# Layer 0 of a hybrid decoder trunk: one block transpose, bonus weights and memory norm in the projection stage, retention scores in banks of two pools

## The chip, the cores and the metric

The kernel runs on one NeuronCore of a Trainium2 chip. The metric is the device time of one execution in microseconds (us), lower is better. Three timed runs of the kernel before gave 912.21, 913.45 and 913.68 us; the median is 913.45 us.

## The reference, cut to what matters

A trunk of two layers over 256 tokens of width 1024. Each layer adds a mixer, a cross-attention into 256 memory tokens and a squared-ReLU MLP; the memory is normalized once, for both layers.

```python
mem_n = rms_norm(mem, mem_norm_w)
h = x
for layer in range(2):
    hn = rms_norm(h, norm_mix_w[layer])
    if layer % 2 == 0:
        proj = hn @ hyb_w_in[i]                       # 1792 columns for A, 2048 for B
        y_a = rwkv7_time_mix(proj[..., :A_COLS], ...)
        y_b = retention(proj[..., A_COLS:], ret_ln_w[i])
        mix = concatenate([y_a, y_b]) @ hyb_w_out[i]
    else:
        mix = diff_attention(hn, ...)
    h = h + mix
    h = h + memory_cross_attention(rms_norm(h, ...), mem_n, ...)
    h = h + squared_relu_mlp(rms_norm(h, ...), ...)
return rms_norm(h, final_norm_w)

def rwkv7_time_mix(pa, ...):                          # 8 heads of 64
    pa = pa + (token_shift(pa) - pa) * mu             # r, k, v, wd, ad, gd are columns of pa
    decay = exp(-exp(-softplus(-(w0 + tanh(wd) @ w2)) - 0.5))
    a = sigmoid(a0 + ad @ a2)
    kk = (k * k_k) / max(norm(k * k_k), 1e-12)        # per head
    k = k * (1 + (a - 1) * k_a)
    y = wkv7_scan(r, decay, k, v, -kk, kk * a)
    y = group_norm(y) + sum(r * k * r_k) * v          # the bonus
    return y * (sigmoid(gd) @ g2)

def retention(pb, ln_w):                              # 8 heads of 64, chunks of 128
    q, k, v, g = split(pb, 4)
    q, k = rotary(q), rotary(k) / 8
    scores = (q @ k.T) * decay_mask                   # inside a chunk; a state crosses chunks
    return rms_norm(scores @ v + cross) * silu(g)
```

## The kernel before, in words

All matrices with weights are multiplied in three passes: a weight piece of 512 KB (`raw`) is loaded by SyncE's queue, ScalarE makes its rounded half `hi` and VectorE the rest `lo` (line 129, `split`), and TensorE multiplies both by the activations' halves (line 121, `mm`). There are four `raw`, three `hi` and three `lo` buffers, so TensorE lets pieces in by finishing older ones.

A tile framework puts every engine's instructions into one fixed order, by priorities and the order of the code; each engine then runs its row of instructions in that order and waits by semaphores. PSUM has eight banks: four in the pool `acc`, two in `mm`, two in `tr`.

Layer 0's mixer, in the order of the code:

- **Start**: `x` is loaded, normalized and transposed to `xT`; the transposes need the identity in `prm` (line 94).
- **Projection stage** (`proj_cols`, seven pairs of blocks): r, k, v, the low-rank inputs; evacuated by `shift_mix`.
- **Vector work of A**: the decays `Ep`, `En`, the vectors `AR`, `bt`, `kt`, the product `rk = r*k` on GpSimd (line 480), its weights `rkb` on GpSimd (line 499), and the bonus `bv` (lines 502 to 505), whose matmul needs both.
- **Projections of B** (`proj_rows` into `acc` banks): k and q with rotary evacuations `rope_evac`, then v, then the gate g.
- **Scores of A** (`scores`): matmuls of `bt` with `AR` in four groups through the `tr` banks, masked by VectorE into `SCb`.
- **Inverse** (`inverse`): the 32x32 diagonal blocks of `SCb` are transposed into `Lc` (line 573, one operation for each quarter of 32 partitions, since the column of the block alternates), scaled by `D2c` (line 576), and inverted by 31 steps of a product and an addition (lines 583, 585), scaled and transposed to `X` (line 588). The recurrence (`solve`) needs `X`.
- **Scores of B** (lines 597 to 617): for four pairs of heads, matmuls of `kTr` and `qTr` into two banks (`ps`, `ps1`), both from `tr`; VectorE masks and ScalarE copies them out to `PT0`, `PT1`.
- **Memory norm** (`load_mem`, called after `inverse`): its weight row is loaded on ScalarE's queue, both memory tiles on SyncE's, squared by ScalarE, scaled by VectorE, transposed by TensorE into `memh`, `meml`.
- **Recurrence of A**: four steps `g`, each a chain over TensorE, VectorE and ScalarE; matmuls of the first cross-attention's keys and values (`kv_chunk`, fed by `memh`, `meml`) are put between.

Of the kernel before, what the change touches and what calls it, by code (L numbers as in the profile page):

```python
# [8 lines left out]
F32 = mybir.dt.float32  # L9
F32R = mybir.dt.float32r  # L10
AF = mybir.ActivationFunctionType
ALU = mybir.AluOpType
# [4 lines left out]
D = 1024  # L17
# [12 lines left out]
R_W0, R_A0, R_KK, R_KA, R_LW, R_LB, R_RK, R_MU, R_RET, R_DIF = (  # L30
    0, 4, 8, 12, 16, 20, 24, 28, 42, 46)
# [6 lines left out]
def kernel(ctx: ExitStack, tc: tile.TileContext, ins: dict, out: bass.AP):  # L38
    nc = tc.nc
    I = ins  # L40
# [5 lines left out]
    const = ctx.enter_context(tc.tile_pool(name="const", bufs=1))  # L46
# [10 lines left out]
    def open_pool(name, side=None):  # L57
        st = ExitStack()
        return st, st.enter_context(tc.tile_pool(name=name, bufs=1, side=side, reuse_waits="tile"))
# [15 lines left out]
    def mm_t():  # L75
        return ps_mm.tile([128, 512], F32, tag="mm", name=nm("mm"))

    def tr_t():
        return ps_tr.tile([128, 512], F32, tag="tr", name=nm("tr"))


    h = glob.tile([128, 2, D], F32, tag="h", name="h")
# [10 lines left out]
    prm = const.tile([128, C_ALL], F32, name="prm")  # L93
# [3 lines left out]
    blk1 = prm[:, C_BO:C_BO + 128]  # L97
# [147 lines left out]
    def scratch():  # L245
        return npool.tile([128, D], F32, tag="xn", name=nm("xn"))
# [45 lines left out]
    def load_row(tl, src, eng):  # L292
        eng.dma_start(out=tl, in_=src.unsqueeze(0).broadcast_to([128, D]))
        return [tl[:, 0:512], tl[:, 512:1024]]
# [33 lines left out]
    def load_mem(pool):  # L328
        mh = pool.tile([128, 8, 256], F32R, tag="memh", name="memh")
        ml = pool.tile([128, 8, 256], F32R, tag="meml", name="meml")  # L330
        row = load_row(kv1pool.tile([128, 2, D], F32, tag="V1", name="memrow")[:, 0, :], I["mem_norm_w"], nc.scalar)

        def src(t):
            mt = scratch()
            nc.sync.dma_start(out=mt, in_=I["mem"][0, t * 128:(t + 1) * 128, :])
            return mt
        norm_T(src, row, mh, ml, (tr_t, tr_t))
        return mh, ml

    def kv_chunk(layer, i, KT, V, between=None):  # L340

        if i < 4:
            def ev(ps):
                if layer == 0:
                    nc.vector.tensor_copy(out=KT[:, 2 * i:2 * i + 2, :], in_=ps)
                else:
                    split(KT[0][:, 2 * i:2 * i + 2, :], KT[1][:, 2 * i:2 * i + 2, :], ps)
            proj_cols(I["w_k"][layer], 2 * i, memT, ev, between=between)
        else:
            c = i - 4  # L350
            proj_rows(I["xattn_w_kv"][layer], D + c * 512, memT,
                      lambda ps, t: nc.scalar.activation(V[:, t, c * 512:(c + 1) * 512], ps, AF.Copy), mm_t)
# [6 lines left out]
    omu = const.tile([128, 14], F32, name="omu")  # L359
    behind(nc.vector.tensor_scalar(omu, prm[:, R_MU:R_MU + 14], -1.0, 1.0, op0=ALU.mult, op1=ALU.add), d1[1], "the activations first")  # L360
    oka = const.tile([128, 4], F32, name="oka")
    const.tile([128, 24], F32, name="pad")
    behind(nc.vector.tensor_scalar(oka, prm[:, R_KA:R_KA + 4], -1.0, 1.0, op0=ALU.mult, op1=ALU.add), d1[1], "the activations first")

    st_pr, prep = open_pool("prep", "right")
    w2a2 = prep.tile([128, 512], F32, tag="w2a2", name="w2a2")

# [3 lines left out]
    r_ = t4(prep, "r")  # L371
# [23 lines left out]
    for b0 in (12, 4, 6, 0, 2, 8, 10):  # L395
        if b0 == 6:
            nc.sync.dma_start(out=w2a2[0:64, :], in_=I["rwkv_w2"][0])
            nc.sync.dma_start(out=w2a2[64:128, :], in_=I["rwkv_a2"][0])
            nc.sync.dma_start(out=prm[:, C_BO:C_ALL], in_=I["c_pack"][:, C_BO:C_ALL])
        if b0 == 8:  # L400
            nc.sync.dma_start(out=g2, in_=I["rwkv_g2"][0])
            nc.sync.dma_start(out=rkt.rearrange("p a t c -> p (a t c)"), in_=I["c_rk"])
        def ev(ps, b0=b0):
            for j in range(2):
                shift_mix(ps[:, j, :], b0 + j)
        proj_cols(I["w_hyb"], b0, xT, ev)

    sg = t4(prep, "sg")  # L410
# [59 lines left out]
    nc.vector.tensor_tensor(kk, kk, a_, op=ALU.mult)  # L470
    nc.vector.tensor_tensor(bt, g16(kk), En, op=ALU.mult)
    for b in range(4):
        nc.vector.tensor_scalar(a_[:, b, :], a_[:, b, :], prm[:, R_KA + b:R_KA + b + 1], oka[:, b:b + 1],
                                op0=ALU.mult, op1=ALU.add)
    nc.vector.tensor_tensor(k_, k_, a_, op=ALU.mult)
    kt_ = pA.tile([128, 16, 64], F32, tag="kt", name="kt")
    nc.vector.tensor_tensor(kt_, g16(k_), En, op=ALU.mult)
    nc.vector.tensor_tensor(AR[:, :, 1, :], g16(r_), Ep[:, :, 1:65], op=ALU.mult)
    rk = r_
    nc.gpsimd.tensor_tensor(rk, r_, k_, op=ALU.mult)  # L480


    def tok_major(src, tag):
# [10 lines left out]
    kT = tok_major(kt_.rearrange("p (b g) t -> p b (g t)", b=4), "kT")  # L494


    rkb = prep.tile([128, 4, 128], F32, tag="sg", name="rkb")
    for b in range(4):
        nc.gpsimd.tensor_scalar(rkb[:, b, :], blk1, prm[:, R_RK + b:R_RK + b + 1], None, op0=ALU.mult)
    bv = v_  # L500
    for b0 in (0, 2):
        ps = tr_t().rearrange("p (b t) -> p b t", b=2)
# [4 lines left out]

    st_rp, rp = open_pool("rp")
    st_pr.close()
    st_mem, mempool = open_pool("mem", "right")  # L510
    st_kv1, kv1pool = open_pool("kv1", "right")
    st_pB, pB = open_pool("pB", "right")
    qkR = [rp.tile([128, 2, 512], F32, tag=f"qk{i}", name=f"qkR{i}") for i in range(2)]
# [10 lines left out]
    def rope_evac(i):  # L524
        def ev(ps, t):
            p4 = ps.rearrange("p (h x d) -> p h x d", h=8, x=2)
            cs, sn = rope_tabs(i, t)
            dst = qkR[i][:, t, :].rearrange("p (h x d) -> p h x d", h=8, x=2)
            tm = scratch()[:, :512].rearrange("p (h x d) -> p h x d", h=8, x=2)
            for x in range(2):  # L530
                nc.vector.tensor_tensor(dst[:, :, x, :], p4[:, :, x, :], cs, op=ALU.mult)
                nc.vector.tensor_tensor(tm[:, :, x, :], p4[:, :, 1 - x, :], sn, op=ALU.mult)
            nc.vector.tensor_tensor(dst[:, :, 0, :], dst[:, :, 0, :], tm[:, :, 0, :], op=ALU.subtract)
            nc.vector.tensor_tensor(dst[:, :, 1, :], dst[:, :, 1, :], tm[:, :, 1, :], op=ALU.add)
        return ev

    wh_in = I["hyb_w_in"][0]
# [28 lines left out]
    def inverse():  # L566

        Lc = pB.tile([128, 32, 32], F32, tag="Lc", name="Lc")
        SCb16 = SCb.rearrange("p a h t -> p (a h) t")
        for q in range(4):  # L570
            pr = slice(q * 32, q * 32 + 32)
            c0 = (q % 2) * 32
            nc.vector.transpose(Lc[pr].rearrange("p t s -> p (t s)"),  # L573
                                SCb16[pr, :, c0:c0 + 32].rearrange("p h t -> p t h").unsqueeze(2)
                                .broadcast_to([32, 32, 2, 16]))
        nc.vector.tensor_tensor(Lc, Lc, D2c.unsqueeze(1).broadcast_to([128, 32, 32]), op=ALU.mult)
        Xc = pB.tile([128, 32, 16], F32, tag="Xc", name="Xc")
        behind(nc.sync.dma_start(out=Xc.rearrange("p s m -> p (s m)"), in_=I["c_xi"]), last_load[0], "weights first")
        for k in range(31, 0, -1):
            m0 = k // 2  # L580
            n = 16 - m0
            pd = pB.tile([128, 32, 16], F32, tag="pd", name=nm("pd"), bufs=1)
            nc.vector.tensor_tensor(pd[:, 0:k, 0:n], Lc[:, k, 0:k].unsqueeze(2).broadcast_to([128, k, n]),
                                    Xc[:, k:k + 1, m0:16].broadcast_to([128, k, n]), op=ALU.mult)
            nc.vector.tensor_tensor(Xc[:, 0:k, m0:16], Xc[:, 0:k, m0:16], pd[:, 0:k, 0:n], op=ALU.add)
        nc.vector.tensor_tensor(Xc, Xc, D2p.unsqueeze(1).broadcast_to([128, 32, 16]), op=ALU.mult)
        X = pB.tile([128, 16, 32], F32, tag="pd", name="X")
        nc.vector.transpose(X.rearrange("p h (m par) -> p m par h", par=2), Xc.rearrange("p s m -> p m s"))
        Xt[0] = X
# [11 lines left out]
    for hq in range(2):  # L601
        p0 = rp.tile([128, 4, 256], F32, tag=f"qk{hq}", name=nm("PT0"))
        p1 = PT1[hq]
        PT0.append(p0)
        for h2 in range(2):
            pr = slice(h2 * 64, h2 * 64 + 64)
            ps = tr_t().rearrange("p (h c) -> p h c", h=2)
            ps1 = tr_t()[:, :256].rearrange("p (h c) -> p h c", h=2)
            for i in range(2):
                hp = 2 * hq + i  # L610
                mm(ps[:, i, :], lhsT=kTr[pr, hp, 0:128], rhs=qTr[pr, hp, :], start=True, stop=True)
                mm(ps1[:, i, :], lhsT=kTr[pr, hp, 128:256], rhs=qTr[pr, hp, 128:256], start=True, stop=True)
            d0 = p0.rearrange("p (i h) c -> p h i c", i=2)[:, h2]
            d1 = p1.rearrange("p (i h) c -> p h i c", i=2)[:, h2]
            nc.vector.tensor_tensor(d0[:, :, 0:128], ps[:, :, 0:128], cmb, op=ALU.mult)
            nc.scalar.activation(d0[:, :, 128:256], ps[:, :, 128:256], AF.Copy)
            nc.vector.tensor_tensor(d1, ps1, cmb, op=ALU.mult)
# [3 lines left out]
        nc.vector.tensor_tensor(gR[:, t, :], ps, gR[:, t, :], op=ALU.mult)  # L621

    inverse()
    memT = load_mem(mempool)
    proj_rows(wh_in, A_COLS + 1536, xT, g_evac, acc_t)
    pos = []
    for t in range(2):
# [671 lines left out]
```

## Time and profile before

| | us |
|---|---|
| median of three runs | 913.45 |
| the profiled execution | 913.95 |
| its span on the core | 912.1 |
| TensorE busy in the span | 885.7 |
| VectorE busy | 601.0 |
| ScalarE busy | 450.7 |
| mean granted TensorE clock | 0.983 of 2.4 GHz |

Times in the views are microseconds from the span's start. "PE" is TensorE's matmuls, "PEld" its weight loads, DVE is VectorE, ACT ScalarE, POOL GpSimd, SP the queue that issues loads. A releaser is the instruction whose end let a waiting one start. A PE that is marked busy can still run slowly: the column PEclk gives the granted share of 2.4 GHz, and 0.50 is 1.2 GHz.

### The profile page before, as it was taken

To read this page: it belongs to the slowest core of one execution; us is meant where nothing else is said; L and a number is where in the kernel's file an instruction comes from. 1 tells how busy PE (TensorE), PEld (TensorE's weight loads), DVE (VectorE), ACT (ScalarE), POOL (GpSimd) and SP (SyncE) were. 2 spreads that over 40 slices of the span, in tenths; PEclk is the share of its full clock that TensorE was granted. 3 is DMA by queue.
4 is the path that set the end of the run, shared out by engine and by line. 5 is a ranking of instruction groups with operands and counts; after the bars stand their busy time and mean duration, and the time that the engine had idled before them with its cause. 6 is when DMAs were issued, how large, how long until landed. Compare 5 with 4: busy or idle time off the path is not lost.

```text
span 912.1 us, 14133 instructions
## 1 busy us (share of the span) xinstructions
PE 885.7 (97%) x5546; PEld 757.8 (83%) x5546; DVE 601.0 (66%) x954; ACT 450.7 (49%) x721; POOL 34.9 (4%) x44
## 2 busy tenths in 40 slices
PE   7998989999999999999999999999999999999996
PEld 5986869877889988888888889878899788888885
DVE  4568868745558557666666674887776666666665
ACT  4754425213556445544444454665465454444443
POOL 1003001000000000000000000001000000000001
PEclk8999969999999999999999999999999999999999
DMA  8544523222465565655655555444453465656551
GB/s 295 183 139 150 162 72 121 87 94 76 134 217 202 155 194 194 197 188 191 193 191 186 189 181 187 138 131 147 139 208 105 127 207 185 189 192 195 187 187 67
DMA packets 47078, 149.98 MB, mean 164 GB/s; under 512 B 4731, under 2 KB 4900, under 8 KB 46884
## 3 DMA queue, kind: packets, MB, share of 16 engines
q1 hardware_dynamic: 45456, 142.73, 48.4%
q10 hardware_dynamic: 1108, 3.72, 1.2%
q0 software_dynamic: 448, 2.63, 0.9%
q8 instruction: 43, 0.70, 0.3%
q14 instruction: 23, 0.19, 0.1%
HBM read 148.01 MB, written 2.63 MB: 165 GB/s over the span
## 4 chain that ended last, share of the span: by engine, by line
PE 89%; DVE 5%; issue 2%; ACT 2%; POOL 1%; DMA 1%; SPq 0%; POOLq 0%; ACTq 0%; DVEq 0%
PE mm L121 37%; PE acc L121 34%; PE tr L121 15%; DVE lo L129 1%; ACT hi L129 1%; DVE Lc L573 1%; DMA prm<-in_c_pack_dram 1%; PE tr L254 1%; PE tr L1104 1%; PE tr L951 1%; DVE z L1085 0%; PE acc L254 0%; DVE xn L268 0%; POOL xn L1182 0%; POOL rs L226 0%
## 5 line engine op out<-in xcount | busy, mean ns | idle before, releaser
L129 DVE TENSOR_TENSOR lo<-raw,hi 128x1024 fp32r<-128x1024 f32 x262 | 320.1, 1224 | 220.9 <-ACT hi L129 219.1
L129 ACT ACTIVATE hi<-raw 128x1024 fp32r<-128x1024 f32 x262 | 277.5, 1060 | 345.6 <-PE mm L121 130.3
L121 PE MATMUL mm<-xhl,hi 128*128 128x256 f32 (+1 forms) x784 | 188.0, 319 | 1.0 <-ACT xhl L129 0.7
L121 PEld LDWEIGHTS mm<-xhl,hi 128*128 128x128 f32 x784 | 129.6, 189 | 11.9 <-ACT xhl L129 1.7
L121 PE MATMUL mm<-xhl,lo 128*128 128x256 f32 x512 | 138.1, 282 | 0.0
L121 PE MATMUL acc<-hi,hl 128*128 128x512 f32 x256 | 100.2, 391 | 0.0
L121 PE MATMUL acc<-hi,hh 128*128 128x512 f32 x256 | 100.1, 391 | 0.0
L121 PE MATMUL acc<-lo,hh 128*128 128x512 f32 x256 | 99.6, 389 | 0.0
L121 PEld LDWEIGHTS mm<-xhl,lo 128*128 128x128 f32 x512 | 96.6, 189 | 2.5
L121 PE MATMUL tr<-xhl,hi 128*128 128x512 f32 x256 | 92.8, 395 | 0.0
L121 PE MATMUL acc<-hi,xhl 128*128 128x512 f32 x256 | 81.9, 396 | 0.0
L121 PE MATMUL tr<-xhl,lo 128*128 128x256 f32 x256 | 66.7, 281 | 0.0
L121 PEld LDWEIGHTS acc<-hi,hl 128*128 128x128 f32 x256 | 48.1, 188 | 11.3 <-DVE hl L129 0.9
L121 PEld LDWEIGHTS acc<-lo,hh 128*128 128x128 f32 x256 | 48.1, 188 | 10.4
L121 PEld LDWEIGHTS acc<-hi,xhl 128*128 128x128 f32 x256 | 47.7, 188 | 9.7
L121 PEld LDWEIGHTS acc<-hi,hh 128*128 128x128 f32 x256 | 48.1, 188 | 8.8
L121 PEld LDWEIGHTS tr<-xhl,hi 128*128 128x128 f32 x256 | 48.2, 188 | 8.5
L121 PEld LDWEIGHTS tr<-xhl,lo 128*128 128x128 f32 x256 | 48.2, 188 | 2.9
L121 PE MATMUL acc<-lo,xhl 128*128 128x512 f32 x128 | 50.4, 394 | 0.0
L121 PE MATMUL mm<-memh,hi 128*128 128x256 f32 x128 | 36.5, 286 | 1.3 <-ACT xhl L132 1.3
L121 PE MATMUL mm<-meml,hi 128*128 128x256 f32 x128 | 37.1, 290 | 0.0
L121 PE MATMUL mm<-memh,lo 128*128 128x256 f32 x128 | 36.6, 286 | 0.0
(299 smaller groups left out, 1393.3 us busy)
## 6 DMA issues: line engine op xcount, KB each, us to landing
raw<-in_w_dram SPq DMA_DIRECT2D x64, 512.0 KB, 3.5
raw<-in_mlp_w_dram SPq DMA_DIRECT2D x64, 512.0 KB, 3.5
raw<-in_hyb_w_in_dram SPq DMA_DIRECT2D x16, 512.0 KB, 3.8
raw<-in_w_k_dram SPq DMA_DIRECT2D x16, 512.0 KB, 3.5
raw<-in_xattn_w_kv_dram SPq DMA_DIRECT2D x16, 512.0 KB, 3.4
raw<-in_w_q_dram SPq DMA_DIRECT2D x16, 512.0 KB, 4.4
raw<-in_xattn_w_o_dram SPq DMA_DIRECT2D x16, 512.0 KB, 3.4
raw<-in_w_dqk_dram SPq DMA_DIRECT2D x16, 512.0 KB, 3.4
```

The costliest lines, as they stand in the source:

```text
L121: ins = nc.tensor.matmul(o, lhsT=lhsT, rhs=rhs, start=start, stop=stop)
L129: return nc.scalar.activation(hi, src, AF.Copy), nc.vector.tensor_tensor(lo, src, r32(hi), op=ALU.subtract)
L254: nc.tensor.transpose(ps[:, k4, :], x[:, kt * 128:(kt + 1) * 128], ident)
L573: nc.vector.transpose(Lc[pr].rearrange("p t s -> p (t s)"), SCb16[pr, :, c0:c0 + 32].rearrange("p h t -> p t h").unsqueeze(2) .broadcast_t ...
L951: nc.tensor.transpose(pt[:, j, m, :], P[:, j, m * 128:(m + 1) * 128], ident)
L1104: nc.tensor.transpose(pt[:, k * 128:(k + 1) * 128], z3[:, 0, k * 128:(k + 1) * 128], ident)
```

## The change

Six edits, all in layer 0, with the same result for the kernel's output:

1. `load_mem` is called inside the projection stage, behind the fourth pair of blocks, and the memory's weight row goes to a buffer of the pool `prep` that is free from the start. The pool `mem` is opened earlier.
2. `rkb` is made by GpSimd inside the projection stage; `rk = r*k` moves from GpSimd to VectorE.
3. The scaling of `a` by k_a (four operations) moves from VectorE to ScalarE; so do the four copies that evacuate the keys of the first cross-attention (`KT`).
4. The rotary evacuation has one multiplication of 512 columns in place of two of 256 and one addition in place of two; the sign is folded into the sine products.
5. In `inverse` ScalarE and VectorE first gather the diagonal blocks into `Ld` with two masks of ones and zeros (`quad`), and one transpose of 128 partitions replaces four of 32.
6. In the scores of B `ps` comes from the pool `mm`, `ps1` from `tr` as before.

```diff
@@ load_mem
-        row = load_row(kv1pool.tile([128, 2, D], F32, tag="V1", name="memrow")[:, 0, :], I["mem_norm_w"], nc.scalar)
+        row = load_row(prep.tile([128, D], F32, tag="kk", name="memrow"), I["mem_norm_w"], nc.scalar)
@@ kv_chunk
-                    nc.vector.tensor_copy(out=KT[:, 2 * i:2 * i + 2, :], in_=ps)
+                    nc.scalar.activation(KT[:, 2 * i:2 * i + 2, :], ps, AF.Copy)
...
+    quad = const.tile([128, 2], F32, name="quad")
+    for q in range(4):
+        for j in range(2):
+            nc.gpsimd.memset(quad[q * 32:q * 32 + 32, j:j + 1], float(q % 2 == j))
...
+    st_mem, mempool = open_pool("mem", "right")
     st_pr, prep = open_pool("prep", "right")
@@ the loop over b0 of the projection stage
         proj_cols(I["w_hyb"], b0, xT, ev)
-
+        if b0 == 0:
+            memT = load_mem(mempool)
+        if b0 == 2:
+
+            rkb = prep.tile([128, 4, 128], F32, tag="rkb", name="rkb")
+            for b in range(4):
+                nc.gpsimd.tensor_scalar(rkb[:, b, :], blk1, prm[:, R_RK + b:R_RK + b + 1], None, op0=ALU.mult)
...
-        nc.vector.tensor_scalar(a_[:, b, :], a_[:, b, :], prm[:, R_KA + b:R_KA + b + 1], oka[:, b:b + 1],
-                                op0=ALU.mult, op1=ALU.add)
+        nc.scalar.activation(a_[:, b, :], a_[:, b, :], AF.Identity, scale=prm[:, R_KA + b:R_KA + b + 1],
+                             bias=oka[:, b:b + 1])
...
-    nc.gpsimd.tensor_tensor(rk, r_, k_, op=ALU.mult)
+    nc.vector.tensor_tensor(rk, r_, k_, op=ALU.mult)
...
-    rkb = prep.tile([128, 4, 128], F32, tag="sg", name="rkb")
-    for b in range(4):
-        nc.gpsimd.tensor_scalar(rkb[:, b, :], blk1, prm[:, R_RK + b:R_RK + b + 1], None, op0=ALU.mult)
@@ rope_evac
+            nc.vector.tensor_tensor(dst, p4, cs.unsqueeze(2).broadcast_to([128, 8, 2, 32]), op=ALU.mult)
             for x in range(2):
-                nc.vector.tensor_tensor(dst[:, :, x, :], p4[:, :, x, :], cs, op=ALU.mult)
-                nc.vector.tensor_tensor(tm[:, :, x, :], p4[:, :, 1 - x, :], sn, op=ALU.mult)
-            nc.vector.tensor_tensor(dst[:, :, 0, :], dst[:, :, 0, :], tm[:, :, 0, :], op=ALU.subtract)
-            nc.vector.tensor_tensor(dst[:, :, 1, :], dst[:, :, 1, :], tm[:, :, 1, :], op=ALU.add)
+                nc.vector.scalar_tensor_tensor(tm[:, :, x, :], p4[:, :, 1 - x, :], 2.0 * x - 1.0, sn,
+                                               op0=ALU.mult, op1=ALU.mult)
+            nc.vector.tensor_tensor(dst, dst, tm, op=ALU.add)
@@ inverse
-        for q in range(4):
-            pr = slice(q * 32, q * 32 + 32)
-            c0 = (q % 2) * 32
-            nc.vector.transpose(Lc[pr].rearrange("p t s -> p (t s)"),
-                                SCb16[pr, :, c0:c0 + 32].rearrange("p h t -> p t h").unsqueeze(2)
-                                .broadcast_to([32, 32, 2, 16]))
+
+        Ld = pB.tile([128, 16, 32], F32, tag="pd", name="Ld", bufs=1)
+        nc.scalar.activation(Ld, SCb16[:, :, 0:32], AF.Identity, scale=quad[:, 0:1])
+        nc.vector.scalar_tensor_tensor(Ld, SCb16[:, :, 32:64], quad[:, 1:2], Ld, op0=ALU.mult, op1=ALU.add)
+        nc.vector.transpose(Lc.rearrange("p t s -> p (t s)"),
+                            Ld.rearrange("p h t -> p t h").unsqueeze(2).broadcast_to([128, 32, 2, 16]))
@@ scores of B
-            ps = tr_t().rearrange("p (h c) -> p h c", h=2)
+            ps = mm_t().rearrange("p (h c) -> p h c", h=2)
             ps1 = tr_t()[:, :256].rearrange("p (h c) -> p h c", h=2)
...
     inverse()
-    memT = load_mem(mempool)
     proj_rows(wh_in, A_COLS + 1536, xT, g_evac, acc_t)
```

The edits also move instructions of each engine. First place: VectorE from the third mask of A's scores to the first masks of B's scores (`PT`). `xn`, `memrow` belong to the memory norm, `lo` to the weight pieces, `pd` and `Xc` to the 31 steps. Before:

```order
L562 TENSOR_TENSOR SCb<-tr_1029,prm 128x512
L268 SCALAR_TENSOR_TENSOR xn_1263<-xn_1261,rs_1270,memrow 128x512
L573 STREAM_TRANSPOSE Lc<-SCb 32x1024
L129 TENSOR_TENSOR lo_1319<-raw_1317,hi_1318 128x1024
L573 STREAM_TRANSPOSE Lc<-SCb 32x1024 x2
L129 TENSOR_TENSOR lo_1337<-raw_1335,hi_1336 128x1024
L573 STREAM_TRANSPOSE Lc<-SCb 32x1024
L129 TENSOR_TENSOR lo_1355<-raw_1353,hi_1354 128x1024
L615 TENSOR_TENSOR PT_142_1115<-tr_1116,prm 128x2x128
L617 TENSOR_TENSOR PT_795<-tr_1117,prm 128x2x128
L576 TENSOR_TENSOR Lc<-Lc,D2c 128x1024
```

and after (in two pieces; between them stand the rest of the first four pairs of `pd` and `Xc`, rows of the same kind):

```order
L570 TENSOR_TENSOR SCb<-tr_1088,prm 128x512
L581 SCALAR_TENSOR_TENSOR Ld<-SCb,quad,Ld 128x512
L582 STREAM_TRANSPOSE Lc<-Ld 128x1024
L129 TENSOR_TENSOR lo_1320<-raw_1318,hi_1319 128x1024
L584 TENSOR_TENSOR Lc<-Lc,D2c 128x1024
L129 TENSOR_TENSOR lo_1338<-raw_1336,hi_1337 128x1024
L591 TENSOR_TENSOR pd_1220<-Lc,Xc 128x31
L593 TENSOR_TENSOR Xc<-Xc,pd_1220 128x31
```

```order
L593 TENSOR_TENSOR Xc<-Xc,pd_1229 128x28x2
L129 TENSOR_TENSOR lo_1356<-raw_1354,hi_1355 128x1024
L623 TENSOR_TENSOR PT_156_1174<-mm_1175,prm 128x2x128
L625 TENSOR_TENSOR PT_862<-tr_1176,prm 128x2x128
L623 TENSOR_TENSOR PT_156_1174<-mm_1184,prm 128x2x128
L625 TENSOR_TENSOR PT_862<-tr_1185,prm 128x2x128
```

Four transposes became one, the scaling of `Lc` and four pairs of steps moved ahead of the first masks, and two pairs of heads are masked in a row.

Second place: TensorE around the first two pairs of heads of B's scores (`acc` are the matmuls of the gate's projection). Before, the second pair comes eleven `acc` matmuls behind the first:

```order
L121 MATMUL acc_1040<-hi_1096,xl_124 128x512
L121 MATMUL tr_1116<-qkT_793,qkT_794 128x256
L121 MATMUL tr_1117<-qkT_793,qkT_794 128x128
L121 MATMUL tr_1116<-qkT_793,qkT_794 128x256
L121 MATMUL tr_1117<-qkT_793,qkT_794 128x128
L121 MATMUL acc_1315<-hi_1318,xh_123 128x512
```

and after, two pairs follow each other, then three `acc` matmuls, then the other two pairs:

```order
L121 MATMUL acc_1099<-hi_1155,xl_124 128x512
L121 MATMUL mm_1175<-qkT_860,qkT_861 128x256
L121 MATMUL tr_1176<-qkT_860,qkT_861 128x128
L121 MATMUL mm_1175<-qkT_860,qkT_861 128x256
L121 MATMUL tr_1176<-qkT_860,qkT_861 128x128
L121 MATMUL mm_1184<-qkT_860,qkT_861 128x256
L121 MATMUL tr_1185<-qkT_860,qkT_861 128x128
L121 MATMUL mm_1184<-qkT_860,qkT_861 128x256
L121 MATMUL tr_1185<-qkT_860,qkT_861 128x128
L121 MATMUL acc_1316<-hi_1319,xh_123 128x512
L121 MATMUL acc_1316<-lo_1320,xh_123 128x512
L121 MATMUL acc_1316<-hi_1319,xl_124 128x512
```

What moved: the four pairs are packed into two bunches, and a third pair meets a bank that the first one still holds.

Third place: SP's queue of loads in the projection stage (`xn` are the memory tiles). After:

```order
L144 DMA raw_336<-in_w_hyb_dram 128x1024
L335 DMA xn_469<-in_mem_dram 128x1024
L144 DMA raw_366<-in_w_hyb_dram 128x1024
L144 DMA raw_401<-in_w_hyb_dram 128x1024
L144 DMA raw_431<-in_w_hyb_dram 128x1024
L335 DMA xn_496<-in_mem_dram 128x1024
L144 DMA raw_524<-in_w_hyb_dram 128x1024
```

Before, the two memory loads stood among the gate's weights, some twenty loads later; the load of `memrow`, which was behind `kT`'s copies on ScalarE's queue, is now the first instruction of that queue.

## Rows read from the trace of the kernel before

**Rows 1.** The page, busy us of each engine (share) and count.
```profile
PE 885.7 (97%) x5546; PEld 757.8 (83%) x5546; DVE 601.0 (66%) x954; ACT 450.7 (49%) x721; POOL 34.9 (4%) x44
```

**Rows 2.** Stretches: length, busy by engine (x instructions), granted clock, DMA share, GB/s.
```profile
14.63:54.90 40.27, 40.27 (x326) 40.27 (x327) 22.93 (x29) 23.93 (x38) 0.00 (x0) 0.96 0.66 211
...
99.20:114.36 15.16, 15.12 (x114) 12.04 (x113) 13.26 (x15) 6.20 (x10) 0.57 (x1) 1.00 0.39 129
118.22:133.72 15.50, 15.50 (x39) 11.33 (x40) 8.50 (x25) 2.44 (x5) 0.00 (x0) 0.50 0.21 69
...
158.87:173.46 14.59, 12.21 (x177) 11.19 (x178) 13.27 (x38) 5.52 (x9) 0.00 (x0) 1.00 0.32 109
```

**Rows 3.** Waits of PE, 50 to 260 us: total, times, longest.
```profile
PE tr L121 <- ACT PT L616: 3.9, 1, 3.9
PE tr L121 <- POOL rkb L499: 2.6, 1, 2.6
PE mm L121 <- ACT xhl L132: 1.3, 1, 1.3
PE tr L121 <- DVE X L588: 0.8, 1, 0.8
```

**Rows 4.** The chain that ended last: start, us, what, count.
```profile
3.54 6.34 DMA prm<-in_c_pack_dram
...
84.22 2.45 PE tr L121 x8
86.66 6.50 PE acc L121 x28
...
118.22 2.93 PE tr L121 x8
```

**Rows 5.** A stretch at the start, columns as in rows 2.
```profile
2.00:4.00 2.00, 2.00 (x6) 0.76 (x5) 0.00 (x0) 0.88 (x4) 0.04 (x1) 1.00 0.92 320
```

**Rows 6.** ScalarE's DMA queue, 80 to 100 us: packets, MB, engines' share.
```profile
q10 hardware_dynamic: 144, 0.52, 8.3%
```

**Rows 7.** Timeline of ACT: the ninth weight piece; a memory square.
```profile
33.65 1.05 ACT L129 ACTIVATE hi<-raw 128x1024 fp32r<-128x1024 f32 x1
...
101.68 0.63 ACT L238 ACTIVATE xn<-xn 128x512 f32<-128x512 f32 x1 [1.78 <-DMA xn<-in_mem_dram]
```

**Rows 8.** Timeline of DVE from the last mask of A's scores.
```profile
104.57 0.68 DVE L562 TENSOR_TENSOR SCb<-tr,prm 128x512 f32<-128x512 f32 x1
...
105.83 2.01 DVE L573 STREAM_TRANSPOSE Lc<-SCb 32x1024 f32<-32x1024 f32 x1
107.78 1.17 DVE L129 TENSOR_TENSOR lo<-raw,hi 128x1024 fp32r<-128x1024 f32 x1
...
114.26 1.90 DVE L573 STREAM_TRANSPOSE Lc<-SCb 32x1024 f32<-32x1024 f32 x1
...
117.33 0.42 DVE L615 TENSOR_TENSOR PT<-tr,prm 128x256 f32<-128x256 f32 x1
...
121.77 0.21 DVE L583 TENSOR_TENSOR pd<-Lc,Xc 128x30 f32<-128x30 f32 x1
...
172.19 1.13 DVE L588 STREAM_TRANSPOSE X<-Xc 128x512 f32<-128x512 f32 x1
```

**Rows 9.** Timeline of POOL: start, duration, line, operation, tiles.
```profile
78.10 5.47 POOL L480 TENSOR_TENSOR r<-r,k 128x1024 f32<-128x1024 f32 x1 [68.58 <-DVE k L475]
83.55 2.36 POOL L499 TENSOR_SCALAR rkb<-prm 128x128 f32<-128x128 f32 x4
```

**Rows 10.** Timeline of PE: two-column matmuls; the first pair of heads.
```profile
60.44 1.88 PE L121 MATMUL tr<-prm,kk 128*128 128x2 f32 x16
...
110.03 1.57 PE L121 MATMUL tr<-qkT,qkT 64*128 64x256 f32 x8
```

**Rows 11.** Stretches around a fall of the clock, columns as in rows 2.
```profile
58.00:62.40 4.40, 4.19 (x27) 3.55 (x27) 3.35 (x4) 4.21 (x9) 0.00 (x0) 1.00 0.70 221
62.40:65.80 3.40, 3.40 (x13) 2.90 (x13) 2.55 (x8) 1.07 (x1) 0.00 (x0) 0.50 0.00 0
```

More of the change, by code (lines that the diff above doesn't have):

```diff
@@ L361 @@
     oka = const.tile([128, 4], F32, name="oka")
-    const.tile([128, 24], F32, name="pad")
+    const.tile([128, 22], F32, name="pad")
+    quad = const.tile([128, 2], F32, name="quad")
+    for q in range(4):
+        for j in range(2):
+            nc.gpsimd.memset(quad[q * 32:q * 32 + 32, j:j + 1], float(q % 2 == j))
     behind(nc.vector.tensor_scalar(oka, prm[:, R_KA:R_KA + 4], -1.0, 1.0, op0=ALU.mult, op1=ALU.add), d1[1], "the activations first")
+    st_mem, mempool = open_pool("mem", "right")
     st_pr, prep = open_pool("prep", "right")
@@ L509 @@
     st_pr.close()
-    st_mem, mempool = open_pool("mem", "right")
     st_kv1, kv1pool = open_pool("kv1", "right")
```

## The prediction

> **What bounds the kernel now.** I read the busy times first: TensorE is busy 885.7 us of a span of 912.1, VectorE 601.0 [rows 1]. TensorE is the bound, and a change that leaves its matmuls as they are can only win where TensorE idles or runs at half clock. The stretches come next [rows 2]: the projection stage (14.63 to 54.90) has no idle time on TensorE; A's and B's scores (99.20 to 114.36) have a VectorE that is busy 13.26 us of 15.16; the next 15.50 us run at a granted clock of 0.50 (1.2 GHz) with TensorE marked busy throughout; the last stretch has 2.38 us of idle. The waits say who ended the idle time [rows 3]: of 50 to 260 us the four longest are 3.9 (the copy out of a head pair's bank), 2.6 (the bonus weights), 1.3 and 0.8 us (`X`). The chain of waits gives sizes [rows 4]: a head pair costs 2.93 us at half clock, and 28 dense `acc` matmuls 6.50 us at full clock, 0.232 each. All of this lies in the part that the diff touches; behind it TensorE's row of instructions is the same, so a gain there is kept to the end and nothing later gives it back.
>
> The sum is made against the profiled execution: 913.95 us, a span of 912.1 and 1.85 around it; the median of the runs is 0.5 lower.
>
> **The change part by part.**
>
> *Memory norm early (edit 1).* Three things move. The weight row's load becomes the first DMA of ScalarE's queue, at a time when the DMA engines are already busy at a share of 0.92 [rows 5]; its 0.52 MB took 8.3% of 20 us, or 1.7 us of all the engines, where it stood [rows 6]. `prm`, which took 6.34 us to land and for which TensorE's first transposes wait [rows 4], then shares them. I take +1.7; the ends are 0, if it fills gaps, and +2.5, if besides 1.6 us more of the stream run at half clock, which costs half of them (a mean of 0.96 over 40.27 us [rows 2] says that about 1.6 us are lost so already). The Trainium skill, "DMA: Bandwidth & Descriptors", section "Issuing engines are not separate DMA queues", says that loads from different engines share the same 16 DMA engines and interleave, which speaks against this edit. By that rule the term is the full 1.7; with a queue of its own bandwidth it would be 0 and the sum 1.7 lower; the share of 0.92 agrees with the rule.
> The eight transposes that stood at each memory tile go into a stage where TensorE is never idle, and leave a later stage where they were as much on the path: zero net. Their squares (four of 0.63 us on ScalarE [rows 7]) and some 6 us on VectorE (eight operations of 128x512 at 0.68 [rows 8], and small ones) stand beside 23.93 and 22.93 busy of 40.27 us [rows 2], so there is cover; without it they would cost up to those 6 us. The two tile loads add 1 MB to a stage at a DMA share of 0.66 [rows 2]; their wait on SP is the last rival.
>
> *Bonus weights and r\*k (edit 2).* GpSimd takes 5.47 us for r*k and then 2.36 for the four weights [rows 9]. The wait of 2.6 us goes [rows 3], and the eight matmuls, which took 2.45 us because the weights came one by one [rows 4], need some 1.75 (by eight of the 256-column matmuls, 1.57 us in the head pair with half of them shorter [rows 10]). VectorE makes r*k at the price of a 128x1024 operation, 1.17 us [rows 8]. −3.2; the ends are −2.0 (VectorE's row, now one longer, brings r*k a microsecond late) and −3.3.
>
> *One transpose, two pools (edits 5, 6).* The 3.9 us wait is VectorE's doing: between the last mask of A's scores (104.57) and the first mask of B's (117.33) stand four block transposes of about 2 us [rows 8]. A transpose of 32x1024 takes 2.01, one of 128x512 takes 1.13 [rows 8]: time goes with elements in a partition, so the new 128x1024 takes about 2.1, and three transposes (6 us) go. But the new row also holds, ahead of the first mask, the scaling of `Lc` and eight small steps. I count from the end of A's score matmuls: mask 0.7, `Ld` on ScalarE 0.6 (as the square of 512 columns [rows 7]), its sum on VectorE 0.7, transpose 2.0, three `lo` 3.6, the scaling 1.2, eight steps of 0.25 (0.21 for the smallest [rows 8]) 2.0, mask and copy 0.8, and some 0.5 for hand-overs: 12.1. TensorE meanwhile has 32 `acc` matmuls (7.4), two pairs of 1.5 [rows 10] and three more `acc` (0.7), 11.1 in all, before the third pair needs the first bank. About 1.0 us of waiting stays: −2.9. Ends: −3.9 (no wait) and −1.5 (the `lo` operations wait for their `hi`).
>
> *The clock behind it.* The stretch of 15.50 us at 0.50 [rows 2] began inside that wait and held three pairs of 2.93 us, 1.5 each at full clock [rows 4, 10]. With a wait of 1.0 us instead, I take the clock to stay at 2.4 GHz: half of 15.5, −7.7. The other end is 0 (it falls for as long again).
>
> *The waits at 158.87 to 173.46.* VectorE loses, up to `X`, three transposes (6 us), the memory norm (6) and two copies of keys (1.4 by 0.68 for 512 columns [rows 8]), 13 us of its row; TensorE arrives about 13 us earlier too. `X` came 0.8 us late; the head pairs at half speed also held VectorE up, so I take that wait as gone. The 1.3 us for `xhl` on ScalarE may stay, since a key copy now stands ahead of it. −1.2; ends −2.4 (all gone) and +0.5 (the copy adds its 0.6).
>
> *Other edits (3, 4).* The scaling of `a`, the rotary sums and key copies change engines or join; TensorE waits for none of them now [rows 3]. The four key copies stand among ScalarE's steps of the recurrence: +0.5, ends 0 and +2.4 (four copies of 0.6 on its chain).
>
> Sum: 1.7 − 3.2 − 2.9 − 7.7 − 1.2 + 0.5 = −12.8, so 901.15 for a run like the profiled one, 900.6 by the median.
>
> **The rivals.**
>
> *The clock falls all the same.* For it: at 62.40 the clock fell to 0.50 for 3.40 us behind 4.40 us in which TensorE had idled only 0.21 us but had run small matmuls, sixteen of two columns among them [rows 10, 11]. Packed head pairs, half the rows high, with a wait of 1.0 between them may do the same. Against it: after the 2.6 us wait for the weights and 2.45 us of paced matmuls the 28 that follow take 0.232 each, so the clock was full [rows 3, 4]. A fall costs half of what it covers: 1.7 us for a stay of 3.4 as at 62.40, 3.4 for twice that, 7.7 for one as before. With 3.4: 904.0, and 902 to 908.5 over all. The Trainium skill, "TensorE: Matmul & The Clock Gate", section "A second HAM failure mode: psum-queue depth-cycling", tells of a kernel in which short idles between groups of matmuls that cycle through PSUM banks made the clock swing; that is this place, and 62.40 agrees that no long idle is needed.
>
> *VectorE comes later than I count.* `Lc`'s scaling and eight steps ahead of the masks are 3.2 us that the old row did not have there; if besides each `lo` waits for its `hi`, the third pair waits 2.5 us and `X` moves with it: 900.6 + 1.5 + 1.2 = 903.3.
>
> *The gain is not there.* If the clock falls for as long as before (7.7), the wait stays at 2.5 and the start costs 2.5: 900.6 + 7.7 + 1.5 + 0.8 = 910.6; with the 0.8 and 0.5 us of the `X` stage lost too, 911.9, which is no change.
>
> *Slower: SP's queue.* The second memory load waits for the buffer of the first tile's norm, and every weight load from the ninth on stands behind it. The ninth piece was split at 33.65 [rows 7]; two loads of 0.52 MB at 211 GB/s [rows 2] need 5 us, so it decides if the first norm ends after 28.6. I put that end at 23: the fourth piece is split when TensorE is done with the first (14.63 + 40.27/14 = 17.5, plus 1.05), then two squares of 0.63 and VectorE's rows. If a stall comes, each of its microseconds is lost on TensorE, and a fall of the clock like the old one adds 7.7: a stall of 8 us gives 900.6 + 8 + 7.7 = 916.3, slower. Against it stand more than 5 us of slack.
>
> **How the numbers follow.** The forecast (897 to 903.5): 0.60. The clock falls all the same: 0.20, of which most lies under 907. VectorE later: 0.08. No gain: 0.05. Slower: 0.07. The likeliest gives 900.6. For 8 in 10 I take the forecast's own range, down to 896.5 for the low ends of the start and of the `X` stage together, and the clock rival up to 907.5. A measurement of this kernel tells about 0.2% (1.8 us) from no change: faster is the first three and a little of the fourth, 0.89; same 0.04; slower 0.07.
>
> **What would show it.** Right: a granted clock of 1.00 from the third head pair on, pairs of 1.5 us, a wait of about 1.0 us ahead of the third pair and none for the bonus weights; one transpose of about 2.1 us; a projection stage longer by the memory transposes with TensorE busy all through; its start later by about 1.7 us; no wait for `X`. Wrong: a stretch at 0.50 behind the pairs, idle time in the projection stage before the ninth weight piece, a transpose of 4 us or more, or new waits of TensorE in the recurrence behind ScalarE's key copies.

## The result

The changed kernel takes 897.98 us (median of four runs, 897.5 to 898.8) against 913.57 (912.2 to 915.7) for the kernel before beside it: a ratio of 0.983, with an interval of 0.981 to 0.985. Repeated beside three of its variants it gave 898.14 and 0.983 again. The prediction was 900.6. Two slow executions, 924.2 us with edit 1 alone and 1441.4 us with edit 2 undone, stand outside the ratios and ranges below.

The page of the changed kernel shows TensorE 9.2 us less busy, with the same 5546 instructions [rows 1]:

```profile
PE 876.5 (98%) x5546; PEld 752.6 (84%) x5546; DVE 593.5 (66%) x937; ACT 454.9 (51%) x730; POOL 30.5 (3%) x51
```

The same instructions in less busy time are for the most part the clock; head pairs that overlap, shown below, are a smaller part. The stretches that answer to [rows 2] and [rows 11] (length, busy of PE, PEld, DVE, ACT, POOL, granted clock, DMA share, GB/s) are the projection stage, both sets of scores, the rest of the head pairs with the gate's projection, the stage ahead of `X`, and the two-column matmuls with what follows them:

```profile
15.19:59.66 44.47, 43.81 (x351) 43.25 (x351) 29.19 (x42) 28.44 (x50) 4.00 (x6) 0.96 0.69 225
97.64:112.17 14.53, 14.49 (x116) 11.67 (x115) 12.31 (x20) 5.59 (x7) 0.00 (x0) 1.00 0.37 113
113.02:125.88 12.86, 12.86 (x62) 10.58 (x62) 11.98 (x35) 5.80 (x8) 0.00 (x0) 1.00 0.39 116
141.00:155.26 14.26, 13.83 (x196) 13.01 (x194) 11.33 (x28) 6.16 (x12) 0.00 (x0) 1.00 0.47 148
...
61.60:66.00 4.40, 4.19 (x27) 3.56 (x27) 3.35 (x4) 4.20 (x9) 0.00 (x0) 1.00 0.56 183
66.00:70.00 4.00, 4.00 (x23) 3.34 (x23) 2.62 (x9) 2.23 (x3) 0.00 (x0) 1.00 0.00 0
```

The third line is where the kernel before had 15.50 us at 0.50: it runs at 1.00 throughout. The first has lost 0.66 us of TensorE time to a wait. Behind the two-column matmuls, the same 4.19 busy us of 4.40 as in [rows 11], the clock stayed at 1.00 in this execution where it had fallen to 0.50. The waits of TensorE from 50 to 260 us, which answer to [rows 3], are now four of under a microsecond:

```profile
PE mm L121 <- ACT PT L624: 0.8, 1, 0.8
PE tr L121 <- DVE SCk L570: 0.3, 1, 0.3
PE tr L663 <- DVE xn L656: 0.2, 1, 0.2
PE tr L121 <- ACT sg L434: 0.2, 1, 0.2
```

VectorE around the block transpose, which answers to [rows 8] (start, duration, line, operation):

```profile
102.96 0.75 DVE L581 SCALAR_TENSOR_TENSOR Ld<-SCb,quad,Ld 128x512 f32<-128x512 f32 x1 [0.85 <-ACT Ld L580]
103.74 2.09 DVE L582 STREAM_TRANSPOSE Lc<-Ld 128x1024 f32<-128x1024 f32 x1
...
112.13 0.42 DVE L623 TENSOR_TENSOR PT<-mm,prm 128x256 f32<-128x256 f32 x1
```

One transpose of 128 partitions takes 2.09 us, as long as one of 32 partitions did.

### The profile page after: what moved, and what is told of

It is laid out like the page before. It is cut to its first block, busy times and chain, and to the rows that moved or that the text cites. A ratio compares the mean times of both kernels' runs of the same rounds, so it can differ in the third digit from the quotient of the medians.

```text
span 895.9 us, 14122 instructions
## 1 busy us (share of the span) xinstructions
PE 876.5 (98%) x5546; PEld 752.6 (84%) x5546; DVE 593.5 (66%) x937; ACT 454.9 (51%) x730; POOL 30.5 (3%) x51
## 4 chain that ended last, share of the span: by engine, by line
PE 90%; DVE 4%; issue 2%; ACT 2%; POOL 1%; DMA 1%; POOLq 0%; SPq 0%; DVEq 0%; ACTq 0%
PE mm L121 37%; PE acc L121 35%; PE tr L121 15%; DVE lo L129 1%; PE tr L254 1%; ACT hi L129 1%; DMA h<-in_x_dram 1%; PE tr L1111 1%; PE tr L958 1%; DVE z L1092 0%; PE acc L254 0%; POOL rs L226 0%; DVE xn L268 0%; PE tr L500 0%; POOL xn L1189 0%
## 5 line engine op out<-in xcount | busy, mean ns | idle before, releaser
L121 PEld LDWEIGHTS mm<-xhl,hi 128*128 128x128 f32 x784 | 129.7, 189 | 12.1 <-ACT xhl L129 2.0
L121 PEld LDWEIGHTS acc<-lo,hh 128*128 128x128 f32 x256 | 48.1, 188 | 10.4
```

What stands on the lines that cost most here:

```text
L121: ins = nc.tensor.matmul(o, lhsT=lhsT, rhs=rhs, start=start, stop=stop)
```

## The experiments

Two theories stood against each other. One: the gain is a sum of independent terms, as the prediction added them, and the largest (7.7 us, the clock) belongs to edits 5 and 6. The other: one quantity, the length of TensorE's wait ahead of the head pairs, decides on the clock, and every edit that shortens VectorE's row there takes part in it. A third question was the start of the kernel and what edit 1 costs there. Ratios are to the kernel before, run in turn with each; costs of an undone edit are differences of such ratios, 0.983 being that of the changed kernel.

**Edits 5 and 6 alone**, on the kernel before (the diff of both stands in the section on the change).

> The kernel before with edits 5 and 6 alone (one block transpose, score banks from two pools). Theory: the 3.9 us wait ahead of the head pairs and the 15.5 us at half clock behind it are the work of these two, so the wait falls to 1 to 2.5 us (the memory norm still stands in VectorE's row there), the clock stays at 2.4 GHz through the pairs, and the time falls by about 11.5 us, to 902. Rival: the clock falls behind any wait in that place; then only 3 to 4 us are won, 909.5. The bonus weights' wait of 2.6 us and the half clock at 62.40 stay in both.

Measured: 902.9 us, ratio 0.9865 (0.984 to 0.989), single runs 901.3 to 906.1. Its waits, and the stretch of the head pairs behind:

```profile
PE tr L121 <- POOL rkb L504: 2.5, 1, 2.5
PE mm L121 <- ACT PT L621: 1.5, 1, 1.5
...
```
```profile
118.88:130.00 11.12, 10.35 (x58) 8.39 (x59) 10.01 (x32) 6.26 (x13) 0.55 (x1) 1.00 0.27 86
```

The wait falls from 3.9 to 1.5 us, the clock stays at 1.00 over the pairs, and the size is that of the theory. The rival falls. Behind the wait of 2.5 us for the bonus weights the clock did fall here, for 3.4 us from 87.1.

**Edit 2 alone**, on the kernel before.

> The kernel before with edit 2 alone (bonus weights in the projection stage, r*k on VectorE). Theory: the wait of 2.6 us goes, the eight bonus matmuls take 1.75 in place of 2.45 us, nothing else moves: -3.2, to 910.3. Rival: VectorE's longer row puts r*k late and gives 1 us back: 911.3. The half clock at 62.40 should be as before, since the edit leaves the work in front of it alone.

Measured: 905.3 us, ratio 0.992 (0.989 to 0.994): 7.7 us gained by the ratio, 9 by the medians, where 3.2 were expected, and single runs from 902.5 to 914.7 with a mean granted clock of 0.995 to 0.979. The profiled execution is the slowest of them:

```profile
PE tr L121 <- ACT PT L618: 2.0, 1, 2.0
```
```profile
116.53:132.10 15.57, 15.57 (x40) 11.36 (x41) 9.32 (x22) 2.64 (x5) 0.00 (x0) 0.52 0.21 67
```
```profile
112.45 2.01 DVE L575 STREAM_TRANSPOSE Lc<-SCb 32x1024 f32<-32x1024 f32 x1
...
115.64 0.42 DVE L617 TENSOR_TENSOR PT<-tr,prm 128x256 f32<-128x256 f32 x1
...
116.42 1.93 DVE L575 STREAM_TRANSPOSE Lc<-SCb 32x1024 f32<-32x1024 f32 x1
```

The expectation that nothing else moves was wrong: the scheduler put the fourth block transpose behind the first masks, so the wait at the head pairs shrank from 3.9 to 2.0 us. With that wait the clock falls in the profiled execution, for 17.1 us; in the run at 902.5 us the mean granted clock of 0.995 leaves no room for such a fall. The two runs differ by 12 us, of which this fall is some 8.5 (half of 17.1); the profile has shorter falls elsewhere too.

**Edit 1 alone**, on the kernel before.

> The kernel before with edit 1 alone (memory norm in the projection stage, its weight row as the first load). Theory: +0.6 at the start, +0.7 of idle time at the second memory tile, transposes neutral, -1.4 since two norm operations leave VectorE's row ahead of the block transposes, -0.8 for X, and -1.7 if the clock does not fall at 60 to 66 us because the stage stands 3 us later there: 911 with that, 912.7 without. Rival: the weight row costs 1.7 at the start and the wait ahead of the pairs stays at 3.9: 914 to 915.

Measured: 908.6 us, ratio 0.9945 (0.993 to 0.9965), single runs 907.4 to 915.2, more gain than expected. Its wait and its clock in the profiled execution (915.2 us, the longest of these):

```profile
PE tr L121 <- ACT PT L618: 2.7, 1, 2.7
```
```profile
120.90:138.80 17.90, 17.90 (x46) 13.22 (x47) 10.54 (x32) 3.10 (x5) 0.00 (x0) 0.52 0.29 89
```

The wait is 1.2 us shorter than in the kernel before. Seven of the other runs, at 907.4 to 908.9 us, have a mean granted clock of 0.986 to 0.990 in place of this one's 0.981, so the fall was shorter or absent in them; without a profile of one of them that is an inference.

**The weight row's load later**, in the changed kernel:

```diff
-        row = load_row(prep.tile([128, D], F32, tag="kk", name="memrow"), I["mem_norm_w"], nc.scalar)
+        tl = prep.tile([128, D], F32, tag="kk", name="memrow")
+        behind(nc.scalar.dma_start(out=tl, in_=I["mem_norm_w"].unsqueeze(0).broadcast_to([128, D])), x_split[0], "x first")
+        row = [tl[:, 0:512], tl[:, 512:1024]]
...
+    x_split = d1
```

> The changed kernel with the load of the memory's weight row issued behind the third weight piece's rounding on ScalarE's queue (about 16 us) in place of first. Theory: the start of the stream goes back from 15.2 to 14.6 us, -0.6: 897.4, and the row is there before VectorE asks for it at 22.9. Rival 1, all of the row's DMA time is won: -1.7, 896.3. Rival 2, the row comes late and VectorE's splits of the fifth piece wait for it: 899 or more.

Measured: 899.5 us, ratio 0.983 (0.981 to 0.985): no difference. The start does not come earlier in a way that stands out: the first three-pass matmul begins at 13.7 us here, at 12.9 to 13.9 in the nine profiles of kernels that load the row first, and at 13.2 to 14.5 in the four that load it where the kernel before does. A new wait shows what the row costs in its new place; `gd` is evacuated behind the memory norm on VectorE, and ahead of the norm ScalarE's first square waits for the memory tile:

```profile
PE mm L121 <- DVE gd L398: 1.6, 1, 1.6
```
```profile
21.40 0.63 ACT L238 ACTIVATE xn<-xn 128x512 f32<-128x512 f32 x1 [2.38 <-DMA xn<-in_mem_dram]
```

The norm waits for these squares and not for the row. Where edit 2 is undone, with the row first and the clock at 1.00 over the same 14 to 20 us, the squares start at 19.84 and `gd` is evacuated at 26.01 in place of 27.61, and there is no such wait. So, as these two profiles have it, the row's load beside the tile's delays the tile by about the 1.6 us that TensorE then waits: the price of rival 2 by another way.

**Edit 5 undone** in the changed kernel (four transposes of 32 partitions).

> The changed kernel with edit 5 undone (four block transposes of 32 partitions). Theory: about 3 us more of VectorE stand ahead of the first masks, the wait ahead of the third pair grows from 0.85 to about 3.5 us, and the clock falls behind it: +2.6 and 2 to 7.7 more, 903 to 908. Rival: without a fall 900.6; and if edit 6 alone carries the gain, 898.

Measured: 904.3 us, ratio 0.9885 (0.987 to 0.990), runs 903.3 to 904.8: 5.0 us by the ratios (0.9885 − 0.983, of 914), the theory.

```profile
PE mm L121 <- ACT PT L620: 3.4, 1, 3.4
```
```profile
115.56:124.88 9.32, 9.31 (x28) 7.65 (x29) 5.70 (x23) 2.21 (x4) 0.00 (x0) 0.50 0.20 59
```

**Edit 6 undone** in the changed kernel (`ps` from `tr` again).

> The changed kernel with edit 6 undone (both banks of a head pair from one pool). Theory: a pair needs the banks of the pair before it, so the second pair comes nine acc matmuls behind the first and waits about 1.3 us; pairs no longer run two in a row, 1.5 us each in place of 2.2 for two: +2, 900. Rival 1: the clock falls, 903 to 908. Rival 2: the pools are worth nothing, 898.

Measured: 899.9 us, ratio 0.984 (0.983 to 0.986), 1.2 us above the changed kernel by the ratios; the intervals overlap. The clock keeps 1.00 over the pairs, the second pair waits 0.2 us where 1.3 was expected, and the pairs stand apart, each 1.57 us long:

```profile
108.72 1.57 PE L121 MATMUL tr<-qkT,qkT 64*128 64x256 f32 x8
112.81 1.57 PE L121 MATMUL tr<-qkT,qkT 64*128 64x256 f32 x8 [0.23 <-ACT PT L625]
```

**Head pairs in another order**, two of the same half of partitions in a row, in the changed kernel:

```diff
-    for hq in range(2):
...
-        for h2 in range(2):
+    for h2 in range(2):
+        for hq in range(2):
+            p0, p1 = PT0[hq], PT1[hq]
```

> The changed kernel with the four head pairs in another order: the two pairs that follow each other use the same 64 partitions (the same half of TensorE's rows) and not the two halves in turn. Theory: two pairs in a row took 2.2 us and not twice 1.5 because matmuls on the two halves run beside each other; in the same half they take 3.0, the first bunch eats the wait of 0.85 and the second costs 0.8: 898.8. Rival: the halves have nothing to do with it, two pairs stay at 2.2 us and the time at 898.0.

Measured: 899.6 us, ratio 0.984 (0.982 to 0.985). The 0.8 us cannot be told from nothing by the time, but the trace tells it. Two pairs in the changed kernel, then here:

```profile
108.93 0.70 PE L121 MATMUL mm<-qkT,qkT 64*128 64x256 f32 x2
109.47 0.38 PE L121 MATMUL tr<-qkT,qkT 64*128 64x128 f32 x2
109.69 0.70 PE L121 MATMUL mm<-qkT,qkT 64*128 64x256 f32 x4
110.12 0.49 PE L121 MATMUL tr<-qkT,qkT 64*128 64x128 f32 x4
110.45 0.59 PE L121 MATMUL mm<-qkT,qkT 64*128 64x256 f32 x2
110.89 0.38 PE L121 MATMUL tr<-qkT,qkT 64*128 64x128 f32 x2
```
```profile
110.47 0.70 PE L121 MATMUL mm<-qkT,qkT 64*128 64x256 f32 x2
...
112.97 0.38 PE L121 MATMUL tr<-qkT,qkT 64*128 64x128 f32 x2
```

108.93 to 111.27 is 2.3 us with matmuls of both halves beside each other (the rows x4 are those of two pairs); 110.47 to 113.35 is 2.9 us, one after the other, at a granted clock of 1.00 in both. The halves are the cause.

**Edits 3 and 4 undone** in the changed kernel.

> The changed kernel with edits 3 and 4 undone (the scaling of a and the key copies on VectorE, rotary sums in twice two operations). Theory: TensorE waits for none of them, so the time stays within 0.5 us: 898 to 898.5. Rival: with r*k on VectorE now, the scaling of a and the rotary sums stand ahead of it and bring back part of the bonus wait, and X comes late: 899.5 to 901.

Measured: 898.1 us, ratio 0.982 (0.980 to 0.983), as the theory had it. Together these edits are worth nothing that can be measured.

**The changed kernel again**, with the next three beside it.

> The changed kernel unchanged, beside the three that follow, so that their differences are read on one chip. Theory: a ratio of 0.983 to the kernel before, as at first. Whether the clock falls for some 3 us at 62 to 70 us is a matter of the execution (it did in the profiles of four kernels that have the changed kernel's work there and not in the changed kernel's own), so single runs differ by up to 2 us.

Measured: ratio 0.983 (0.981 to 0.985), runs 897.4 to 900.2. In its profiled execution the clock did fall behind the two-column matmuls, for 3.4 us:

```profile
66.03:69.44 3.41, 3.41 (x13) 2.96 (x12) 1.85 (x5) 0.56 (x1) 0.00 (x0) 0.50 0.00 0
```

So the 1.7 us that the first profile shows as won there are chance, and no edit's doing.

**Steps behind the masks, memory norm one pair of blocks later**, in the changed kernel:

```diff
...
+                if k == 31:
+                    behind(step, mask1[1], "masks first")
...
-        if b0 == 0:
-            memT = load_mem(mempool)
         if b0 == 2:
+            memT = load_mem(mempool)
...
+            mask1.append(nc.vector.tensor_tensor(d1, ps1, cmb, op=ALU.mult))
```

> The changed kernel with two moves: the eight small steps of the inverse go behind the masks of the first two head pairs, and the memory norm is called one pair of blocks later in the projection stage. Theory: the wait of 0.85 us ahead of the third pair goes (VectorE is 2.0 us earlier at the masks, and X has 7 us to spare), and so do the 0.66 us of idle time at the second memory tile: -1.5, ratio 0.981. Rival 1: the third pair then waits for its mm bank behind ScalarE's copy all the same, -0.7. Rival 2: the memory tile meets the busier v blocks and TensorE waits there for 1 us or more: no change.

Measured: 898.9 us, ratio 0.983 (0.981 to 0.985): no gain. The wait ahead of the third pair is gone, but the one at the second memory tile stays, and the waits left are these:

```profile
PE tr L254 <- DVE xn L268: 0.6, 1, 0.6
PE tr L666 <- DVE xn L659: 0.4, 1, 0.4
...
```

Between the first pair and the first use of `PT` it is 0.8 us shorter than the run beside it, and from there to the first use of `X` 0.9 longer, where matmuls of the keys stand in another order. No version beat the changed kernel by more than the intervals.

**Edit 1 undone** in the changed kernel.

> The changed kernel with edit 1 undone (memory norm behind the inverse again). Theory: -0.6 at the start and -0.7 of idle time in the projection stage come back as a gain, but two norm operations of 0.7 us stand ahead of Ld on VectorE again, and the wait ahead of the third pair grows from 0.85 to about 2.2: no change, ratio 0.983, or up to 8 us more in executions in which the clock falls behind the longer wait. Rival: edit 1 is worth 2 us or more without the clock (X, key stage): ratio 0.986.

Measured: 902.1 us, ratio 0.987 (0.985 to 0.989): 3.6 us, above the theory's "no change" and inside its range of up to 8 us.

```profile
PE mm L121 <- ACT PT L623: 1.9, 1, 1.9
```
```profile
114.10:120.90 6.80, 6.80 (x26) 5.50 (x23) 5.01 (x18) 3.18 (x8) 0.26 (x1) 0.50 0.11 44
```

The two norm operations make the wait 1.9 us, and in the profiled execution the clock falls behind it: 3.4 us, half of 6.8. By this profile the time is won at the pairs, not where the memory norm itself runs.

**Edit 2 undone** in the changed kernel.

> The changed kernel with edit 2 undone (r*k and the bonus weights on GpSimd behind it). Theory: the wait of 2.6 us and the paced matmuls come back, 3.2 us, and nothing at the head pairs: ratio 0.9865. Rival, since the kernel before with edit 2 alone gained 9 us: the wait for the weights also makes the clock fall at the pairs, then 8 us or more, ratio 0.992.

Measured: 901.2 us, ratio 0.986 (0.983 to 0.989): 2.4 us, near the theory, though the intervals overlap. The wait at the pairs is 0.9 us as in the changed kernel, and the clock does not fall there, so the rival falls. But the time comes by other waits than the theory's; TensorE, VectorE and TensorE again:

```profile
PE tr L496 <- DVE kt L485: 1.6, 1, 1.6
```
```profile
79.31 2.82 DVE L129 TENSOR_TENSOR lo<-raw,hi 128x1024 fp32r<-128x1024 f32 x1
```
```profile
85.17 3.62 PE L121 MATMUL tr<-r,rkb 128*128 128x256 f32 x8 [0.47 <-ACT kT L497]
```

The wait of 2.6 us for the weights does not come back. GpSimd's r*k ran from 78.64 to 81.04, and the split that VectorE began beside it took 2.82 us in place of 1.22, so `kt` came late. The eight bonus matmuls took 3.62 us in place of 1.97, while the weights came one by one and the clock stood at 0.50 until 88.4.

Together, by the length of the wait ahead of the second or third head pair (whichever has to wait) and the half clock behind it, one profiled execution each:

| kernel | wait, us | at half clock behind it, us |
|---|---|---|
| steps behind the masks | 0 | 0 |
| edit 6 undone; same half; 3 and 4 undone | 0.2; 0.3; 0.6 | 0 |
| changed (twice); row later; edit 2 undone | 0.9 | 0 |
| edits 5 and 6 alone | 1.5 | 0 |
| edit 1 undone | 1.9 | 6.8 |
| edit 2 alone | 2.0 | 17.1 |
| edit 1 alone | 2.7 | 17.1 |
| edit 5 undone | 3.4 | 10.2 |
| before | 3.9 | 17.1 |

No profile with a wait up to 1.5 us shows a fall at the pairs, every profile from 1.9 on does. The stays begin between 1.2 us ahead of the wait's end and 1.4 us behind it. The mean granted clocks of the runs without a profile say that near 2 to 2.7 us it depends on the execution. No run made the wait longer or shorter and changed nothing else: that the wait, and not what comes with it, decides is argued from the order of this table. Elsewhere an equal wait did otherwise: behind the 2.5 to 2.6 us for the bonus weights the clock fell for 3.4 us with edits 5 and 6 alone and with edit 1 alone, and not in the kernel before. Where edit 6 holds, the fall is shorter at an equal wait; the pairs are packed there and dense `acc` matmuls follow sooner. That this is the reason was not tried.

## Why the prediction was right, step by step

The direction, the main mechanism and, within some 3 us, the size held: 12.8 us forecast, 15.6 measured by the medians. Part of the agreement is luck: the start cost 1.1 us less than forecast and the memory norm 1.1 more, and of what was won beyond the forecast 1.7 us are a chance of the execution.

- *Clock, −7.7.* Right: the stretch runs at 1.00, and undoing edit 5 brings a half clock back. But it does not belong to edits 5 and 6 alone. Undone one by one, edit 5 costs 5.0 us, edit 1 3.6, edit 2 2.4 and edit 6 1.2; alone, by the ratios, edits 5 and 6 win 12.3, edit 2 7.7 and edit 1 5.0, 25 together where the whole is 15.6. Edits 1, 5 and 6, and edit 2 on the kernel before, shorten one and the same wait.
- *Wait ahead of the pairs, −2.9 with 1.0 left.* Right: 3.86 became 0.85. The chain counted as 12.1 us took 11.7 (from the end of A's score matmuls at 101.4 to the third pair at 113.0), with the transpose at 2.09.
- *Bonus weights, −3.2.* The wait of 2.6 is gone, and the eight matmuls take 1.97 us in place of 2.45 [rows 4] where 1.75 was forecast: −3.0. Undone it costs 2.4, by other waits.
- *Start, +1.7.* Wrong in size. The sharing is there: the first square of `x` starts at 5.81 us in place of 3.33, as these rows of the changed kernel and the kernel before show,

```profile
5.81 0.63 ACT L238 ACTIVATE xn<-h 128x512 f32<-128x512 f32 x1 [3.14 <-DMA h<-in_x_dram]
```
```profile
3.33 0.63 ACT L238 ACTIVATE xn<-h 128x512 f32<-128x512 f32 x1 [1.11 <-DMA h<-in_x_dram]
```

  but `x` had time in hand. TensorE's first transposes waited for `prm`; in the changed kernel the norm of `x` ends their wait, and no later:

```profile
10.02 1.07 PE L254 MATMUL tr<-prm,xn 128*128 128x128 f32 x8 [4.08 <-DMA prm<-in_c_pack_dram]
```
```profile
9.73 1.97 PE L254 MATMUL tr<-prm,xn 128*128 128x128 f32 x8 [3.06 <-DVE xn L268]
```

  Over all profiles they start at 9.5 to 9.8 us with the row first and at 9.8 to 10.4 without. The stream starts 0.6 us later in this profile since the eight transposes ran at a granted clock of 0.50, in the kernel before at 1.00; the falls at the start differ between executions. Over all profiles the stream starts no later with the row. The step charged the whole DMA time to the path, where the lower end of its range, 0, is what the runs show. The Trainium skill, "DMA: Bandwidth & Descriptors", section "Issuing engines are not separate DMA queues", is borne out for the transfers. The 1.7 us of time were the prediction's own step, and no run shows them.
- *Memory norm in the projection stage, neutral.* Nearly. The stage is 44.47 us long against 41.45 to the same matmul, so the transposes took 2.4 us and 0.66 went to waiting for the second tile's norm; some 2.0 us of transposes are gone later. The cover by 24 us of busy time in 40 was an average: the second tile's squares stand in ScalarE's row behind the copies of the first tile's transposes.
- *Waits ahead of `X`, −1.2.* Too small: 2.38 us of idle time [rows 2] became 0.4, and `xhl` is no longer waited for, in spite of the key copy ahead of it.
- *Other edits, +0.5.* Nothing that can be measured, by the run with 3 and 4 undone.
- *Left out:* the overlap of two packed pairs of opposite halves, some 0.7 us a bunch. It is what edit 6 adds beside the freed bank.

Added up by these readings of the two profiles (0.6 + 0.7 + 2.4 − 2.0 for the memory, −3.0, −3.0, −7.7, −1.4, −1.9, and −1.7 of chance at 62 us) it is −17.0, where the two profiled executions differ by 16.3; 0.7 us are not placed.

Of the rivals, the one that the clock falls all the same did not come about at a wait of 0.85 us. VectorE was not later than counted, and SP's queue did not stall: the first norm ended at 24.3 us, where 23 was forecast and 28.6 was the limit. The Trainium skill, "TensorE: Matmul & The Clock Gate", section "A second HAM failure mode: psum-queue depth-cycling", describes such swings for short idles between groups that cycle through banks; at the packed pairs no run up to a wait of 1.5 us shows it.

## What to carry to other kernels

When an idle gap stands in front of small or half-height matmuls, price the half clock behind it before the gap itself, and ask of every edit whether it shortens that one gap: its gains there need not add up, and half a microsecond on another engine (a wait of 1.5 or of 1.9 us here) can go with several. Test such edits by undoing them from the finished kernel as well as alone, over several executions, since near the point where the clock falls one profile settles little. A load that shares the DMA engines costs only what it adds to the chain that TensorE waits for: nothing for the row as the first load here, 1.6 us for the same row beside a memory tile.

## What the runs showed of the hardware

A block transpose on VectorE takes as long on 32 partitions as on 128 (2.01 and 2.09 us for 1024 elements in a partition). Matmuls of 64 rows in opposite halves of the array run beside each other if they follow each other in TensorE's row (2.3 us for two head pairs against 2.9 in one half). A load of 0.5 MB on ScalarE's queue delayed loads on SyncE's: `x` by 2.5 us at the start, a memory tile by 1.6 us in the stream. GpSimd's r*k, 5.47 us in the kernel before [rows 9], took 2.40 us where edit 2 was undone:

```profile
78.64 2.40 POOL L488 TENSOR_TENSOR r<-r,k 128x1024 f32<-128x1024 f32 x1 [34.84 <-DVE k L483]
```

In the kernel before, VectorE's operations of 128x1024 beside it took 1.2 us each, their usual time; here the split beside it took 2.82 us. So one of the two engines lost what the other kept. Spans on GpSimd are rough, and what decides which one loses was not tried.
